# Weight loads of two attention groups on ScalarE's queue, and no cached-key steps in a group's first two row blocks

## The chip, the cores and the metric

One core of a Trainium2 chip runs the kernel. Its engines are TensorE (PE: matmuls, with its weight loads shown as PEld), VectorE (DVE), ScalarE (ACT), GpSimd (POOL) and SyncE (SP), which here only issues DMAs. Each engine works through its own list of instructions in order and waits where an instruction's operands aren't there. DMAs are issued by SP, ACT or POOL, wait in the issuer's list like any other instruction, and are carried by 16 DMA engines. The metric is the device time of one execution in microseconds, as the median of several runs.

## What is computed

One layer of a decoder on 1024 prompt rows and 8 x 8 sample rows, width 1024, all in float32:

```python
u = rmsnorm(x); a, q, k, v, g_a, g_b = split(u @ w_in)
# branch A: pooling over windows of 2/4/8/16 rows of a, a small linear map, @ w_pa
# branch B: attention in 3 head groups of 4 heads with (window, dilation)
#           (128, 1), (512, 4), (2048, 16); q and k are normed for each head
# a sample row attends to its group's cached keys and values as well:
#           out, lse = dilated_attention_sample(q, [cache_k, k], [cache_v, v], dil, band)
# the three groups' outputs are weighted by their softmax denominators, then @ w_pb
h = x + (sigmoid(g_a) * A + sigmoid(g_b) * B) @ w_o
y = h + relu(rmsnorm(h) @ w_up)**2 @ w_down
```

## The kernel before, in words

Every weight is split into a high and a low part in a reduced float32 form, and a product is made of three matmul passes. A weight panel of 2048 columns is brought by `panel` (L102): four raw pieces of 128 x 512 (256 KB) are loaded (L97 to L100), ScalarE copies the high part into `places` (L93), VectorE subtracts it from the raw piece for the low part (L94). All raw pieces of the kernel share three slots, so a piece can be loaded when the piece three before it has been split and subtracted. `places` holds three panels.

The attention stage runs the head groups in the order 2, 1, 0 (L932). Each group has three panels, for q, k and v, brought by `load(j)` (L959). For groups 1 and 0, `load(0)` and `load(1)` stand at the head of the group (L969, L970), `load(2)` behind the first q parts (L986); their splits are held back until given matmuls have ended, since they overwrite the panels of the group before. The row blocks follow: block 8 (the 64 sample rows) together with block 0, then blocks 1 to 5 alone, then 6 and 7. `qkv_part` (L522) makes q, k or v of a block: matmuls, then on ScalarE the squares for the norms (L557), on GpSimd the power (L561), on ScalarE the scale (L566). The attention of earlier blocks is put between these parts by a hand-written round of generators (`step`, L479).

The samples of group 2 attend to keys that lie 16 rows apart, so that each row has keys of its own. This work is cut into steps by the generator `sample_own_keys` (L733): a step loads a piece of the cache (`piece`, L724, 512 KB in two DMAs), multiplies the piece before it in four GpSimd products (L744 for keys, L768 for values) and reduces on VectorE (L746, or L771 and L772). There are 16 pieces of keys, one step for the softmax, 16 pieces of values, and 35 steps with the first load and the last sum. `own_step(1)` (L979) makes one step behind each part of each prompt block of groups 1 and 0; GpSimd's products are held until the matmuls before them have ended, the loads are not held. The generator's query tile `qs` is set up at the head of group 1 (L948 to L954). A finishing part on the samples (`sample_finish`, L868) starts when all steps are done.

TensorE's order is the program's. For the other engines, and for the queues of DMAs, a planner simulates the program ahead of time and orders the instructions by when they are ready, in the program's order among those that are; a load without a hold is put as early as its tile is free.

Of the kernel before, what the change touches and what calls it, by code (L numbers as in the profile page):

```python
# [10 lines left out]
ALU = mybir.AluOpType  # L11
# [4 lines left out]
P = 128  # L16
# [11 lines left out]
HD = 64  # L28
# [4 lines left out]
def decoder_step(ctx, tc, i, o):  # L33
    nc = tc.nc
    v_, s_, g_, t_ = nc.vector, nc.scalar, nc.gpsimd, nc.tensor
    dma = nc.sync.dma_start
# [60 lines left out]
    def raw_piece(src, name, a, load=dma):  # L97
        raw = rr(wp, [P, 512], F32, name=f"raw_{name}_{a}", tag="raw", bufs=3)
        load(raw, src[:, a:a + 512])
        return raw  # L100

    def panel(src, name, between=None, after=None, ahead=None):  # L102

        n = src.shape[1]
        wt = places[:, place[0] % 3]
        place[0] += 1
        for a in range(0, n, 512):
            raw = ahead.pop(0) if ahead else raw_piece(src, name, a)
            if between is not None:
                between(a // 512)  # L110
            ins = split(wt[:, 0, a:a + 512], wt[:, 1, a:a + 512], raw)
            if after is not None:
                behind_pe(ins, after[a // 512])
        throttle.append(ins)
        return wt
# [31 lines left out]
    new_d = [dp.tile([NT, NB, 768], F32, name=f"new_d{g}") for g in range(3)]  # L147
# [312 lines left out]
    ap = pb.enter_context(tc.tile_pool(name="att", bufs=1, reuse_waits="tile"))  # L460
# [50 lines left out]
    ends_of = {}  # L511
# [387 lines left out]
    own_keys = None  # L899
    count = [0]  # L900

    def own_step(every):
        count[0] += 1
        if count[0] % every == 0:
            if next(own_keys, True) is not None and (2, "own") not in done:
                done.add((2, "own"))
# [25 lines left out]
    for g in (2, 1, 0):  # L932
        nq = i["qk_norm"]
        if g == 1:
            assert ("p", 3) in done
            flush()
            pa.close()
            pam.close()
            ap2 = pb2.enter_context(tc.tile_pool(name="att2", bufs=1, reuse_waits="tile"))
            sp1 = psm.enter_context(tc.tile_pool(name="smp1", bufs=1, side="right", reuse_waits="tile"))  # L940
            np_ = psm2.enter_context(tc.tile_pool(name="nat", bufs=1, side="right", reuse_waits="tile"))
            sp = psm2.enter_context(tc.tile_pool(name="smp2", bufs=1, side="right", reuse_waits="tile"))
            osm = ap2.tile([P, 3, 4, 66], F32, name="osm")

            for a in range(2):
                v_.memset(osm[64:, a], 0.0)
                v_.memset(osm[64:, a, :, 64], -NEG)
            qs = sp1.tile([P, 768], F32, name="qs")  # L948
            for hf in range(2):
                dma(qs[64 * hf:64 * hf + 64], new_d[2].rearrange("t b c -> (t b) c"))  # L950
            wq = sp1.tile([P, 2, 256], F32, name="wq", tag="ss")[:, 0]
            dma(wq, bass.AP(tensor=nq.tensor, offset=nq.offset + 2 * 512, ap=[[0, P], [1, 256]]))
            v_.scalar_tensor_tensor(qs[:, :256], wq, HD ** -0.5, qs[:, :256], op0=ALU.mult, op1=ALU.mult)
            own_keys = sample_own_keys(qs)  # L954
        wrow = ap1.tile([P, 256], F32, name=f"wrow{g}", tag="wrow")
        dma(wrow, bass.AP(tensor=nq.tensor, offset=nq.offset + g * 512 + 256, ap=[[0, P], [1, 256]]))
        wts = [(place[0] + j) % 3 for j in range(3)]

        def load(j, *after):  # L959
            panel(i["w_in"][2 + 3 * j + g], f"qkv{g}_{j}", after=[ends_of[a] for a in after] or None)  # L960


        if g == 2:
            load(0)
            load(1)
            load(2)
        else:
            h = g + 1
            load(0, (h, 6, 1), (h, 7, 1), (h, 6, 2), (h, 6, 2))  # L969
            load(1, (h, 6, 2), (h, 7, 2), (h, 7, 2), (h, 7, 2))  # L970
        for blks in ((8, 0), (1,), (2,), (3,), (4,), (5,)) + (((6, 7),) if g else ((6,), (7,))):
            if g == 1 and 6 in blks:
                in_order(0)
            tiles = {b: qkv_tiles(f"{g}_{b}", b == 8) for b in blks}

            for js in (((0, 1), (2,)) if blks[0] in (1, 2, 3, 4, 5) else ((0,), (1,), (2,))):
                for b in blks:
                    qkv_part(g, wts, b, f"{g}_{b}", tiles[b], js)
                    if g < 2 and b < 8:  # L979
                        own_step(1)  # L980
                    if 2 in js:
                        (sample_block if b == 8 else prompt_block)(g, b, *tiles[b])
                if g == 2 and 2 in js and 8 in blks:
                    start(pool_branch(), "p", now=True)
                if g < 2 and 0 in js and 8 in blks:
                    load(2, (g, 8, 0), (g, 0, 0), (g, 0, 0), (g, 0, 0))  # L986


    while (2, "own") not in done:
# [68 lines left out]
    for d in range(4):  # L1058
# [7 lines left out]
        for u, (c, m) in enumerate(units):  # L1066
# [3 lines left out]
            name = f"{d}_{c}_{m}"  # L1070
# [663 lines left out]
```

## Time and profile before

| | us |
|---|---|
| median of 3 runs (1481.65 to 1486.06) | 1483.24 |
| the profiled execution's own time | 1482.97 |
| its span, first to last instruction | 1481.2 |

Busy shares of the span are 98% for TensorE, 94% for its weight loads, 68% for VectorE, 46% for ScalarE and 28% for GpSimd. A matmul's end is modelled, so a busy TensorE isn't one at its peak. The granted TensorE clock is a share of its full 2.4 GHz; 0.50 is the lower of its two levels, 1.2 GHz, and a mean between them says that part of the stretch was at either. The attention stage lies from about 55 to 430 us of the span: group 2 to about 174, group 1 to about 281, group 0 to about 409. A wait is idle time of an engine just before an instruction, put down to what came last.

### The profile page before, as it was taken

What the parts mean: (1) busy time and instruction counts of PE and PEld (TensorE: products, weight loads), DVE (VectorE), ACT (ScalarE), POOL (GpSimd) and SP (SyncE); (2) the same over time, 40 slices, a digit from 0 to 9 for tenths busy, and PEclk for the clock granted to TensorE, in tenths of its full rate; (3) what the DMA queues carried; (4) which work ended last, traced back from release to release, by engine and by line L of the source; (5) the groups of instructions that cost most, each with busy time, mean ns of one, the idle gap of its engine ahead of it and who ended that gap; (6) DMA issues with size and microseconds to landing.
All of it is one profiled execution on the core that took longest, in us unless ns stands there. A gap on an engine that the chain in (4) does not pass through costs nothing.

```text
span 1481.2 us, 28011 instructions
## 1 busy us (share of the span) xinstructions
PE 1446.0 (98%) x10595; PEld 1397.2 (94%) x10595; DVE 1009.2 (68%) x1949; ACT 687.8 (46%) x1885; POOL 412.5 (28%) x619
## 2 busy tenths in 40 slices
PE   8999899989999999999999999999998999999998
PEld 8988788878999999999998999999998999999998
DVE  7555555767864443434668989888987566777786
ACT  8466745667784222222346665655555322222220
POOL 1611246646500000010200121111224444544430
PEclk9999899999999999999999999999999999999999
DMA  6311767764456547468620777766768788567542
GB/s 216 98 47 63 194 139 174 211 182 119 119 146 201 197 163 258 163 203 287 249 101 27 286 265 265 277 247 254 265 246 306 297 345 322 227 273 277 216 189 113
DMA packets 124277, 304.72 MB, mean 206 GB/s; under 512 B 19111, under 2 KB 72045, under 8 KB 118830
## 3 DMA queue, kind: packets, MB, share of 16 engines
q1 hardware_dynamic: 102334, 192.27, 39.5%
q0 software_dynamic: 21376, 109.88, 20.4%
q8 instruction: 83, 1.36, 0.4%
q10 hardware_dynamic: 432, 0.79, 0.2%
q14 instruction: 52, 0.43, 0.1%
HBM read 218.49 MB, written 128.05 MB: 234 GB/s over the span
## 4 chain that ended last, share of the span: by engine, by line
PE 74%; issue 11%; DVE 5%; DMA 5%; POOL 3%; ACT 2%; SPq 0%; POOLq 0%; ACTq 0%; DVEq 0%
PE p1d L1202 12%; PE pga L136 6%; PE pgb L136 6%; PE pqk L136 6%; PE p2d L1202 6%; PE ph L136 6%; PE p1u L1202 5%; PE pv L136 4%; PE a L264 3%; PE pa L136 3%; PE p3d L1202 3%; PE p2u L1202 2%; POOL z_d L1335 2%; DMA raw_qkv<-in_w_in_dram 2%; DVE places L94 2%
## 5 line engine op out<-in xcount | busy, mean ns | idle before, releaser
L1202 PE MATMUL p1d<-act,places 128*128 128x272 f32 x1104 | 191.3, 288 | 3.9 <-DVE yd L1582 1.4
L1202 PEld LDWEIGHTS p1d<-act,places 128*128 128x128 f32 x1104 | 163.0, 188 | 5.4 <-DVE yd L1582 2.5
L1335 POOL DMA_DIRECT2D z_d<-zs_M x105 | 56.4, 537 | 245.6 <-DVE zs_M L94 242.4
L1632 POOL DMA_DIRECT2D out_kv_sample_dram<-in_cache_kv_dram x44 | 22.1, 505 | 317.6 <-ACT places L93 303.1
L1582 DVE TENSOR_TENSOR yd<-yd,p1d 128x544 f32<-128x544 f32 x116 | 83.1, 716 | 38.5 <-PE p1d L1202 38.4
L93 ACT ACTIVATE places<-sd 128x512 fp32r<-128x512 f32 x64 | 37.4, 625 | 143.7 <-issue 106.9
L1202 PE MATMUL p1u<-t,places 128*128 128x272 f32 x768 | 103.1, 291 | 0.7 <-ACT q L1449 0.7
L1202 PE MATMUL p1u<-act,places 128*128 128x272 f32 x768 | 102.2, 289 | 1.3 <-ACT q L1377 1.3
L1202 PEld LDWEIGHTS p1u<-t,places 128*128 128x128 f32 x768 | 99.7, 191 | 0.8 <-ACT q L1449 0.8
L1202 PEld LDWEIGHTS p1u<-act,places 128*128 128x128 f32 x768 | 98.6, 188 | 1.8 <-ACT q L1377 1.5
L136 PE MATMUL pga<-act,places 128*128 128x384 f32 (+1 forms) x576 | 98.0, 328 | 0.0
L136 PE MATMUL pgb<-act,places 128*128 128x384 f32 (+1 forms) x576 | 97.8, 326 | 0.0
L1202 PE MATMUL p2d<-act,places 128*128 128x272 f32 x528 | 93.9, 288 | 1.6 <-DVE places L94 1.0
L136 PEld LDWEIGHTS pgb<-act,places 128*128 128x128 f32 x576 | 95.4, 188 | 0.0
L136 PE MATMUL ph<-act,places 128*128 128x384 f32 (+2 forms) x624 | 95.4, 314 | 0.0
L136 PEld LDWEIGHTS ph<-act,places 128*128 128x128 f32 x624 | 95.3, 188 | 0.0
L136 PEld LDWEIGHTS pga<-act,places 128*128 128x128 f32 x576 | 94.6, 188 | 0.3
L561 POOL TENSOR_TENSOR mr<-ms,mhalf 128x4 f32<-128x4 f32 (+2 forms) x39 | 51.4, 1319 | 110.9 <-DVE ms L560 105.9
L93 ACT ACTIVATE places<-rd 128x512 fp32r<-128x512 f32 x64 | 37.1, 625 | 94.6 <-PE p1d L1202 94.6
L1202 PEld LDWEIGHTS p2d<-act,places 128*128 128x128 f32 x528 | 78.8, 188 | 2.3 <-DVE places L94 1.2
L1534 POOL TENSOR_TENSOR sd<-rd 128x128 f32<-128x128 f32 x64 | 38.6, 604 | 130.3 <-DVE places L94 115.7
L94 DVE TENSOR_TENSOR zs_M<-q,zs_M 128x544 fp32r<-128x544 f32 x75 | 54.0, 722 | 19.7 <-ACT zs_M L93 19.7
(383 smaller groups left out, 3673.1 us busy)
## 6 DMA issues: line engine op xcount, KB each, us to landing
z_d<-zs_M POOLq DMA_DIRECT2D x105, 544.0 KB, 4.4
act<-z_d SPq DMA_DIRECT2D x73, 544.0 KB
out_kv_sample_dram<-in_cache_kv_dram POOLq DMA_DIRECT2D x36, 960.0 KB, 7.4
ru<-in_w_up_dram SPq DMA_DIRECT2D x16, 1024.0 KB
rd<-in_w_down_dram SPq DMA_DIRECT2D x15, 1024.0 KB
raw_qkv<-in_w_in_dram SPq DMA_DIRECT2D x36, 256.0 KB
zc<-z_d SPq DMA_DIRECT2D x16, 544.0 KB
pck<-in_cache_kv_dram SPq DMA_DIRECT2D x32, 256.0 KB
```

The source lines that it names most:

```text
L93: ins = s_.activation(dst_hi, src, AF.Copy)
L94: v_.tensor_tensor(dst_lo, src, dst_hi.bitcast(F32), op=ALU.subtract)
L136: last_mm[0] = t_.matmul(out, lhs(a, k), rhs(b, k), start=(j == 0), stop=(j == len(terms) - 1))
L264: last_mm[0] = t_.matmul(pts[m][:, :n], wt[:, a, kk, m * P:(m + 1) * P], act4[b][kk][:, :, part4(c)], start=(p == 0 and kk == 0), stop=(p ...
L561: g_.tensor_tensor(r[:n, :H], ms[:n, :H], mhalf[:n, :H], op=ALU.pow)
L1202: last_mm[0] = t_.matmul(pt[:, s, :R4], w(a, k), z(b, k, s), start=(start and j == 0), stop=(j == len(terms) - 1), skip_group_check=True)
L1335: g_.dma_start(z_d[f][AT[m]], st.rearrange("p b l -> p (b l)").bitcast(F32))
L1534: ins = g_.tensor_tensor(s[:, 0], a21, a22, op=ALU.add)
L1582: v_.tensor_tensor(part, part, p[src], op=ALU.add)
L1632: ins = g_.dma_start(d, a)
```

## The change

`panel` takes the function that issues its loads. In groups 1 and 0 the 24 raw pieces of the six panels with a held split are issued by ScalarE instead of SP; group 2 and the later stages stay on SP. The call of `own_step` behind the three parts of block 0 is left out in both groups. One more step is made behind the value parts of blocks 2 and 4 in group 1 and of block 2 in group 0. The loads of `qs` and `wq`, the product on them and the start of the generator move from the head of group 1 to behind the key parts of its first two row blocks (8 and 0); the tiles are still taken at the head.

```diff
-    def panel(src, name, between=None, after=None, ahead=None):
+    def panel(src, name, between=None, after=None, ahead=None, load=dma):
...
-            raw = ahead.pop(0) if ahead else raw_piece(src, name, a)
+            raw = ahead.pop(0) if ahead else raw_piece(src, name, a, load)
...
             qs = sp1.tile([P, 768], F32, name="qs")
-            for hf in range(2):
-                dma(qs[64 * hf:64 * hf + 64], new_d[2].rearrange("t b c -> (t b) c"))
             wq = sp1.tile([P, 2, 256], F32, name="wq", tag="ss")[:, 0]
-            dma(wq, bass.AP(tensor=nq.tensor, offset=nq.offset + 2 * 512, ap=[[0, P], [1, 256]]))
-            v_.scalar_tensor_tensor(qs[:, :256], wq, HD ** -0.5, qs[:, :256], op0=ALU.mult, op1=ALU.mult)
-            own_keys = sample_own_keys(qs)
...
-            panel(i["w_in"][2 + 3 * j + g], f"qkv{g}_{j}", after=[ends_of[a] for a in after] or None)
+            panel(i["w_in"][2 + 3 * j + g], f"qkv{g}_{j}", after=[ends_of[a] for a in after] or None,
+                  load=nc.scalar.dma_start if after else dma)
...
-                    if g < 2 and b < 8:
+                    if g < 2 and 0 < b < 8:
                         own_step(1)
+                        if 2 in js and (g, b) in ((1, 2), (1, 4), (0, 2)):
+                            own_step(1)
...
                 if g < 2 and 0 in js and 8 in blks:
                     load(2, (g, 8, 0), (g, 0, 0), (g, 0, 0), (g, 0, 0))
+                if g == 1 and 1 in js and 8 in blks:
+                    for hf in range(2):
+                        dma(qs[64 * hf:64 * hf + 64], new_d[2].rearrange("t b c -> (t b) c"))
+                    dma(wq, bass.AP(tensor=nq.tensor, offset=nq.offset + 2 * 512, ap=[[0, P], [1, 256]]))
+                    v_.scalar_tensor_tensor(qs[:, :256], wq, HD ** -0.5, qs[:, :256], op0=ALU.mult, op1=ALU.mult)
+                    own_keys = sample_own_keys(qs)
```

## Rows read from the trace of the kernel before

**Rows 1.** TensorE's waits, 150 to 330 us: waiter, releaser: total us, times, longest.
```profile
PE pv L541 <- DVE places L94: 5.0, 4, 3.3
...
PE pv L538 <- ACT places L93: 2.3, 1, 2.3
PE sg1b L597 <- ACT ocg1b L631: 2.3, 1, 2.3
...
PE pq L541 <- DVE places L94: 2.0, 2, 1.4
...
PE pos L855 <- DMA vts<-in_cache_kv_dram: 1.5, 1, 1.5
...
PE tps L828 <- DVE pxs L822: 1.0, 1, 1.0
...
PE pog1b L628 <- ACT pTg1b L619: 0.7, 1, 0.7
```

**Rows 2.** Windows: length, busy us of PE, PEld, DVE, ACT, POOL; clock, DMA share, GB/s.
```profile
150.00:162.00 12.00, 12.00 (x99) 11.39 (x98) 5.89 (x20) 10.14 (x41) 2.02 (x2) 1.00 0.42 114
162.00:174.00 12.00, 12.00 (x106) 11.74 (x105) 7.86 (x23) 8.67 (x35) 1.88 (x2) 1.00 0.90 257
...
177.00:188.00 11.00, 6.02 (x27) 4.45 (x26) 4.87 (x11) 7.59 (x40) 2.42 (x3) 0.50 0.75 195
188.00:192.00 4.00, 4.00 (x24) 4.00 (x25) 1.08 (x9) 1.65 (x8) 0.00 (x0) 0.68 0.00 0
...
299.00:304.00 5.00, 5.00 (x30) 4.97 (x30) 3.59 (x16) 4.27 (x24) 1.78 (x2) 0.66 0.95 254
...
192.00:262.00 70.00, 70.00 (x542) 58.36 (x541) 39.14 (x116) 38.28 (x197) 39.33 (x49) 1.00 0.73 171
```

**Rows 3.** TensorE in time order: start, duration, instruction, count, [idle before <- releaser].
```profile
171.22 3.14 PE L136 MATMUL pk<-places,act 128*128 128x256 f32 x24
176.69 0.45 PE L538 MATMUL pv<-places,smp_t 128*128 128x256 f32 x1 [2.33 <-ACT places L93]
...
409.07 2.34 PE L136 MATMUL pga<-act,places 128*128 128x384 f32 x12
...
430.82 0.63 PE L896 MATMUL sft<-cst,sres 128*128 128x64 f32 x4
```

**Rows 4.** SP in time order; runs of one kind are merged, waits between them included.
```profile
152.38 8.79 SPq L99 DMA_DIRECT2D raw_qkv<-in_w_in_dram  x5
...
165.34 1.40 SPq L950 DMA_DIRECT2D qs<-new_d  x2
...
169.34 1.54 SPq L99 DMA_DIRECT2D raw_qkv<-in_w_in_dram  x3
...
177.99 7.56 SPq L99 DMA_DIRECT2D raw_qkv<-in_w_in_dram  x4
```

**Rows 5.** VectorE in time order.
```profile
163.45 0.69 DVE L94 TENSOR_TENSOR places<-raw_qkv,places 128x512 fp32r<-128x512 f32 x1
...
304.09 2.49 DVE L822 TENSOR_TENSOR pxs<-ps,cst 128x32 f32<-128x32 f32 x1 [0.94 <-ACT ps L817]
...
397.91 0.89 DVE L776 TENSOR_TENSOR osm<-osm,ss 128x256 f32<-128x256 f32 x2
```

**Rows 6.** The chain that ended last, in time order, pieces of loads: start, us, what.
```profile
159.36 3.17 DMA raw_qkv<-in_w_in_dram
...
169.34 6.65 DMA raw_qkv<-in_w_in_dram
...
177.99 5.83 DMA raw_qkv<-in_w_in_dram
```

**Rows 7.** Loads issued by ScalarE at the start: ns least/median/most, first and last start.
```profile
L99 ACTq DMA_DIRECT2D raw_a<-in_w_in_dram x3: 412/451/452, 0.7 to 1.7; - x3
```

**Rows 8.** GpSimd in time order.
```profile
221.91 5.59 POOL L744 TENSOR_TENSOR pck<-pck,qs 128x256 f32<-128x256 f32 x8 [5.96 <-DMA pck<-in_cache_kv_dram]
...
304.20 2.33 POOL L768 TENSOR_TENSOR pcv<-pcv,sc 128x256 f32<-128x256 f32 x4
```

## The prediction

> **What bounds the kernel now.** The page's busy shares put TensorE far ahead of the rest, so time can only be won where TensorE waits or runs at its lower clock. The list of who waited for whom, cut to the stretch of the three attention groups, names seven groups of waits [rows 1]; in the time order of TensorE all of them lie at the two changes of group, about 174 to 186 us and 281 to 318 us. Between these, from 192 to 262 us, TensorE is busy for 70.00 of 70 us [rows 2], while steps on the cached keys run all the time. So the change is worth what it does to two stretches, and can cost something in the blocks between them.
>
> *First change of group (2 to 1).* The key part of block 0 starts at 171.22 us and takes 3.14, to 174.36; the value part of the sample block starts at 176.69 after a wait of 2.33 for the split of the third panel [rows 3]. With the waits inside that part it is 2.3 + 5.0 = 7.3 us [rows 1]. The granted clock is 0.50 from 177 to 188 us and 0.68 to 192 us [rows 2]: the lower level of the two, after a stretch with waits. At half clock TensorE's 6.02 busy us hold 3.0 us of work, so 3.0 are lost, and 4.0 x 0.32 = 1.3 after that. Sum: **11.6 us**.
>
> Why is the panel late? Its first three pieces go out from 169.34 us, in SP's order behind the loads of qs (165.34), of two norm rows and of a cache piece [rows 4]. The slot of the first was free at 164.14, when VectorE had subtracted the piece three before it (163.45 + 0.69) [rows 5]: 5.2 us lost in SP's order. Then the load took 6.65 us, against 3.17 for the same size ten us earlier; the fourth piece needs the first one's slot, goes out at 177.99 and takes 5.83 [rows 6]. The DMA engines are busy at 0.90 in 162 to 174 us [rows 2].
>
> *Second change (1 to 0).* Five waits: 2.0 + 2.3 + 1.5 + 1.0 + 0.7 = 7.5 us [rows 1], and 5 us at clock 0.66 [rows 2], 1.7 lost: **9.2 us**. Together at most 20.8 us are to be had.
>
> **Part 1: 24 weight pieces go from SP's queue to ScalarE's.** At the first change the first piece no longer stands behind SP's loads. It is out at 164.14 + 0.45, the duration of the same load issued by ScalarE at the kernel's start [rows 7]. Landing takes 3.17 to 6.65 [rows 6]: 167.8 to 171.2. Split and subtraction are some 0.7 each (0.69 for the second [rows 5]; the first is taken as equal), so the slot is free at 169.2 to 172.6; the fourth piece is out 0.45 later, takes 3.17 to 5.83, and with its own 1.4 it is there at 174.2 to 180.3. TensorE wants it three quarters into a sample part: 16 matmuls at the rate of 24 in 3.14 [rows 3] are 2.1 us, so at 174.36 + 1.6 = 175.9. A wait of 0 to 4.4 us stays. I take 2.0, about the middle, since the engines stay nearly full but the queue is no longer shared, and suppose that the clock doesn't fall for so little. Gain 11.6 - 2.0 = **9.6** (7.2 to 11.6).
>
> The rows show a piece that takes 6.65 us behind other loads of its queue and 3.17 before them [rows 6]; that it is the queue is my reading. The Trainium skill (DMA: Bandwidth & Descriptors, "Issuing engines are not separate DMA queues") speaks against it: DMAs of all issuing engines run on the same 16 DMA engines, and another issuer saves only the time of issuing. By that rule the pieces keep 6.65 and 5.83 and the gain is 7.2 in place of 9.6. No row here shows two such queues at once.
>
> What the edit adds lies on ScalarE: 24 issues x 0.45 = 10.8 us [rows 7], half in each change of group. ScalarE is busy for 10.14 + 8.67 = 18.8 of the 24 us from 150 to 174 [rows 2], which leaves 5.2 us for the 9 issues that fall there (4.1). They hide, barely; without that cover they cost up to 5.4 in each change. Each issue also waits in ScalarE's order for its slot, and behind it stand the norms' squares and scales, the exponentials and the copies out of PSUM, for which TensorE's transposes and products wait. I charge **0.5**; the case where these waits are long is a rival below. On SP nothing is added, and what stood behind its weight loads goes out earlier.
>
> **Part 2: no steps in blocks 8 and 0 of groups 1 and 0, one more at three later blocks.** A step is four GpSimd products, 5.59 / 2 = 2.8 us [rows 8], a VectorE pass and a 512 KB load (two SP issues). 35 steps are needed. Before there are 19 calls in each group, three of them at block 0; after there are 18 and 17, so the last step comes with the last block of group 0.
>
> At the second change VectorE's product of the sample's probabilities takes 2.49 us from 304.09 on, for a 128x32 operand [rows 5], beside GpSimd's products of 304.20 to 306.53 [rows 8]: it waits there rather than works. With the step gone, TensorE's 1.0 behind it goes. The two waits behind ScalarE (2.3 and 0.7) come of ScalarE standing in front of a raw piece; two value loads leave that stretch, so pieces land sooner, but the waits for slots come to ScalarE. I take half of 2.3 + 0.7 + 1.7 (clock): 2.4. The 2.0 of the first panel stays (blocks 6 and 7 keep their steps just before it), and the 1.5 for a load of cached values. Gain **3.4** (-2 to 9.2; below nothing if the 5.4 us of issues all lie in the way).
>
> The cost: the steps crowd. At the three blocks with an added step two come at once. The nearest row is a pair that already runs without a gap, eight products in 5.59 us at 221.91 [rows 8], in the stretch where TensorE waits for nothing [rows 2]. Bounds 0 and, if TensorE stands for one step at each, 3 x 2.8 = 8.4; I take **0.5**, near the row.
>
> The end: the sum over the cached values was done at 397.91 + 0.89 [rows 5] and TensorE reads what comes of it at 430.82 [rows 3]. It now waits for the last block, whose end is near 409.07, where the first gate begins [rows 3]; with a step's 2.8 us and VectorE's sums it still has some 15 us of cover: nothing. qs is set up behind the sample's key part and is wanted only in block 1: nothing; without that cover its loads would hold GpSimd's first products, not TensorE.
>
> **Sum.** 9.6 + 3.4 - 0.5 - 0.5 = 12.0 us off the profiled execution, 1482.97 us (span 1481.2 and 1.8 around it), which is 0.3 below the median of 1483.24: **1471 us**. Late next are the fourth piece of group 1's third panel and the first panel of group 0. The gates and the MLP behind are TensorE's own chain and move forward as they are.
>
> **The rivals.**
> *Bandwidth, not the queue (the change doesn't clear the way).* The planner sends loads that have no pace as early as it can, so qs and two cache pieces may still fill 162 to 177 us although their step stands later in the program. For it: the share of 0.90 [rows 2]. Against it: the 5.2 us in SP's order go in any case. 7.2 in group 1, nothing in group 0, 1.0 of cost: 6.2 off, 1476.8.
> *Crowded steps.* GpSimd waits for a load between paired steps, the norms' power behind it is late, and TensorE stands at three blocks: 1471 + 8.4, about 1479.4, within 0.3%. Against it: the pair of [rows 8].
> *ScalarE held (slower).* An issue waits for its slot in ScalarE's own order. On SP five issues took 8.79 us at 152.38, and four 7.56 us at 177.99 [rows 4]; without some 0.34 each for the issues that is 7.1 + 6.2 = 13.3 us of waiting in one change of group. If ScalarE sits there, with 5.4 of issues it needs 18.7 us and has 5.2: 13.5 late, past the 11.6 to be won, and in group 0 the same 13.5 against 9.2. Sum 1.9 + 4.3 = 6.2 slower, about 1489. It decides once ScalarE waits for slots for more than some 11 us in each change. Against it: on SP, pieces that nothing hurried made most of that waiting.
>
> **How the numbers follow.** Forecast 0.55 (its own range 1464 to 1478), bandwidth 0.20, crowded steps 0.12, ScalarE held 0.13. A measurement of this kernel can tell about 0.3%, 4.4 us, from no change; faster is below 1478.8. Of the four cases 0.54, 0.15, 0.04 and 0 lie there: 0.73. Within: 0.01 + 0.05 + 0.07 + 0.03 = 0.16. Slower: 0.01 + 0.10 = 0.11. The range goes from 20 us off (nearly all of the 20.8) into the crowded case: 1463 to 1481.
>
> **What would show it.** Right: no fall of the granted clock at 177 us; weight pieces issued by ScalarE within 0.5 us of their slot; the sample's value part within 2 us of the key part's end; no GpSimd products in the first two blocks of groups 1 and 0; TensorE without waits from block 1 on. Wrong: raw pieces that still take 6 us; ScalarE idle in front of issues; norms' scales late behind paired steps.

## The result and the profile after

The changed kernel takes 1495.75 us (median of 6 runs, 1490.67 to 1496.91) where the kernel before took 1483.74 beside it (1479.98 to 1486.06): a ratio of 1.0081, with an interval of 1.0065 to 1.0097. It is slower, by some 12 us, where 12 us of gain were forecast. The profiled execution's span went from 1481.2 to 1495.1 us.

Where the time came is read best from the drift of TensorE: the start of the same matmuls in both traces, after less before. The first place lies ahead of the change; the five others cut the stretch into the parts that the prediction priced.

| start of | before, us | after, us | drift | part that ends there | its share |
|---|---|---|---|---|---|
| value parts of blocks 6 and 7, group 2 | 153.6 | 153.9 | +0.3 | all that comes before | +0.3 |
| value part of block 0, group 1 | 187.9 | 187.0 | -0.9 | first change of group | -1.2 |
| value part of block 7, group 1 | 277.7 | 283.5 | +5.8 | blocks of group 1 | +6.7 |
| value part of block 1, group 0 | 324.8 | 330.1 | +5.3 | second change of group | -0.5 |
| value part of block 7, group 0 | 405.5 | 413.6 | +8.1 | blocks of group 0 | +2.8 |
| the samples' sums (L896) | 430.8 | 445.0 | +14.1 | end of attention, first gates | +6.0 |

Each drift is that of one execution. At 153.6 us, ahead of all edits, the traces of the kernels shown below differ by up to 1.1 us from that of before, and this is taken off the first share. after and after_short (below), whose edits are alike up to block 6 of group 0, differ by 1.5 us in their first share, so a share under some 2 us in one kernel alone isn't read.

TensorE's waits of after from 150 to 440 us answer to [rows 1] (waiter, releaser: total us, times, longest):

```profile
PE pv L541 <- DVE places L94: 7.0, 2, 4.9
PE pos L855 <- DMA vts<-in_cache_kv_dram: 3.0, 2, 2.1
PE sg1b L597 <- ACT ocg1b L631: 2.4, 1, 2.4
PE pog1b L628 <- ACT pTg1b L619: 1.9, 1, 1.9
PE tpg0b L616 <- ACT ocg0b L631: 1.8, 1, 1.8
PE tcg0b L720 <- DVE ocg0b L654: 1.5, 1, 1.5
PE sg1b L597 <- DVE ps L815: 1.4, 1, 1.4
```

The wait for the split of the third panel is still there (7.0 in place of 5.0 and 2.3). New are the one behind ps, one more for a load of cached values, and those for tpg0b and tcg0b. That of pog1b has grown from 0.7 to 1.9, and the one behind pxs is gone. The windows of after answer to [rows 2] (length, busy us of PE, PEld, DVE, ACT, POOL; clock, DMA share, GB/s):

```profile
162.00:174.00 12.00, 12.00 (x106) 11.74 (x104) 6.04 (x18) 7.52 (x26) 1.00 (x1) 1.00 0.91 259
174.00:188.00 14.00, 6.31 (x37) 5.03 (x36) 8.64 (x34) 10.61 (x56) 3.01 (x3) 0.73 1.10 215
192.00:262.00 70.00, 66.42 (x488) 54.44 (x487) 35.57 (x107) 34.65 (x185) 37.02 (x47) 0.98 0.56 146
...
400.00:440.00 40.00, 36.21 (x284) 34.43 (x284) 30.11 (x103) 28.59 (x91) 15.58 (x20) 0.96 0.53 141
```

The stretch from 192 to 262 us, which had been full [rows 2], has lost 3.6 us of work; at the end, where GpSimd is busy for 15.58 us, TensorE stands for 3.8 of 40. The DMA share in 162 to 174 us is 0.91, as it was (0.90).

*The first change of group.* The third panel in after; ACTq and SPq are the two issuers of DMAs:

```profile
166.60 0.33 ACTq L99 DMA_DIRECT2D raw_qkv<-in_w_in_dram  x1
...
169.03 2.00 SPq L798 DMA_DIRECT2D kts<-in_kT_dram  x2
...
173.08 1.99 SPq L730 DMA_DIRECT2D pck<-in_cache_kv_dram  x2
173.09 0.63 ACT L93 ACTIVATE places<-raw_qkv 128x512 fp32r<-128x512 f32 x1 [4.07 <-DMA raw_qkv<-in_w_in_dram]
...
174.52 0.34 ACTq L99 DMA_DIRECT2D raw_qkv<-in_w_in_dram  x1
...
176.65 0.37 SPq L798 DMA_DIRECT2D kts<-in_kT_dram  x1
177.13 2.27 SPq L730 DMA_DIRECT2D pck<-in_cache_kv_dram  x2
...
182.94 0.63 ACT L93 ACTIVATE places<-raw_qkv 128x512 fp32r<-128x512 f32 x1 [1.02 <-DMA raw_qkv<-in_w_in_dram]
...
184.35 0.47 PE L541 MATMUL pv<-places,smp_t 128*64 128x256 f32 x1 [4.90 <-DVE places L94]
```

The first piece goes out at 166.60 in place of 169.34 [rows 4] and lands 6.5 us later, at 173.09; the fourth goes out at 174.52 and takes 8.4 us, with TensorE behind it. Beside them SP sends three loads of the samples' keys and two cached pieces (four DMAs), though the steps that the pieces belong to now stand a block later: nothing holds loads, and the planner still puts them here. In before the two pieces had gone out 5 to 6 us earlier, all ahead of the fourth piece (177.99 [rows 4]):

```profile
167.89 1.35 SPq L730 DMA_DIRECT2D pck<-in_cache_kv_dram  x2
...
170.96 0.60 SPq L730 DMA_DIRECT2D pck<-in_cache_kv_dram  x1
```

Now the fourth piece, 3.5 us earlier itself, is under way together with them.

*The blocks of group 1.* What the first added step, behind the value part of block 2, leads to:

```profile
219.75 5.60 POOL L744 TENSOR_TENSOR pck<-pck,qs 128x256 f32<-128x256 f32 x8 [4.37 <-PE sg1b L597]
...
223.87 7.35 SPq L730 DMA_DIRECT2D pck<-in_cache_kv_dram  x4
...
228.77 2.81 POOL L744 TENSOR_TENSOR pck<-pck,qs 128x256 f32<-128x256 f32 x4 [3.42 <-DMA pck<-in_cache_kv_dram]
231.61 1.22 DVE L746 TENSOR_REDUCE sc<-pck 128x16 f32<-128x1024 f32 x1 [0.60 <-POOL pck L744]
232.72 0.98 SPq L846 DMA_DIRECT2D vts<-in_cache_kv_dram  x2
232.75 0.29 DVE L815 TENSOR_TENSOR ps<-pss,ps 128x136 f32<-128x136 f32 x1
...
233.09 0.71 PE L597 MATMUL sg1b<-qkTg1b 64*128 64x128 f32 x6 [1.44 <-DVE ps L815]
```

There are two slots for cached pieces. The two steps use up both pieces that are there, eight products without a gap (219.75). The next piece goes out only at 223.87, when the slot of the first of them has come free; SP sends its two DMAs and the two of the piece behind it, the last when the second slot comes free, and sits there for 7.35 us with the samples' value loads behind it (232.72). GpSimd waits 3.42 us for the next step's piece; VectorE's sum of it stands in VectorE's order ahead of the samples' scores (L815), for which TensorE waits, by now in block 4. Behind the pair at block 4 the value loads are late again: TensorE waits 2.14 us for one at 254.07, in block 5.

*The end.* GpSimd and ScalarE in after:

```profile
417.71 2.53 POOL L768 TENSOR_TENSOR pcv<-pcv,sc 128x256 f32<-128x256 f32 x4 [2.36 <-DMA pcv<-in_cache_kv_dram]
420.20 1.00 POOL L561 TENSOR_TENSOR mr<-ms,mhalf 128x4 f32<-128x4 f32 x1
...
421.24 0.93 ACT L566 ACTIVATE qk<-pk,mr 128x64 f32<-128x64 f32 x4 [3.27 <-POOL mr L561]
```

The last step's products wait 2.36 us for their piece and stand in GpSimd's order ahead of the power for the norms of the last block (mr); ScalarE waits 3.27 us for that, and the last block's attention, transposes and exponentials all come later. VectorE's order is in the way too: the product that tcg0b waits for (L654) starts at 417.64, straight behind a sum of the steps (L772, 417.04 to 417.72).

### The profile page after: what moved, and what is told of

Its sections match the earlier page's. It is cut to its first block, busy times and chain, and to the rows that moved or that the text cites. A ratio compares the mean times of both kernels' runs of the same rounds, so it can differ in the third digit from the quotient of the medians.

```text
span 1495.1 us, 28003 instructions
## 1 busy us (share of the span) xinstructions
PE 1451.7 (97%) x10595; PEld 1400.4 (94%) x10595; DVE 1009.3 (68%) x1949; ACT 686.4 (46%) x1885; POOL 412.6 (28%) x619
## 4 chain that ended last, share of the span: by engine, by line
PE 60%; issue 18%; DMA 6%; POOL 6%; DVE 5%; ACT 3%; SPq 0%; POOLq 0%; ACTq 0%; DVEq 0%
PE p1d L1206 11%; PE ph L136 6%; PE pgb L136 6%; PE pga L136 6%; PE p2d L1206 5%; PE pqk L136 4%; POOL z_d L1339 3%; PE a L264 3%; PE pv L136 3%; PE pa L136 3%; PE p3d L1206 2%; DMA raw_qkv<-in_w_in_dram 2%; PE pb L136 2%; DVE places L94 1%; DMA pck<-in_cache_kv_dram 1%
## 5 line engine op out<-in xcount | busy, mean ns | idle before, releaser
L93 ACT ACTIVATE places<-s_M 128x512 fp32r<-128x512 f32 x64 | 40.1, 628 | 57.9 <-PE p1u L1206 32.7
```

What stands on the lines that cost most here:

```text
L93: ins = s_.activation(dst_hi, src, AF.Copy)
```

## The experiments

All runs are set against the kernel before on the same chip. The drift of each at the six places, in us:

| kernel | 153.6 | 187.9 | 277.7 | 324.8 | 405.5 | 430.8 | median against before | ratio, interval |
|---|---|---|---|---|---|---|---|---|
| after | +0.3 | -0.9 | +5.8 | +5.3 | +8.1 | +14.1 | 1495.75, 1483.74 | 1.0081 [1.0065, 1.0097] |
| queue_only | +1.1 | +0.3 | +1.2 | -0.4 | -0.4 | -0.6 | 1481.02, 1481.86 | 0.9992 [0.9977, 1.0007] |
| steps_only | +0.1 | -2.7 | +6.0 | +6.0 | +9.7 | +14.9 | 1496.66, 1481.86 | 1.0096 [1.0067, 1.0124] |
| steps_g1 | -0.3 | -4.0 | +1.5 | +0.4 | +0.5 | +3.1 | 1489.45, 1481.86 | 1.005 [1.0032, 1.0068] |
| after_hold | -0.2 | -4.1 | +5.1 | +6.1 | +7.9 | +11.9 | 1493.54, 1481.86 | 1.0086 [1.0067, 1.0104] |
| g1_nodouble | +0.4 | -4.5 | -4.9 | -3.4 | -3.3 | +0.8 | 1483.32, 1482.42 | 1.0007 [0.9994, 1.0019] |
| doubles_only | -0.7 | -1.7 | +5.1 | +2.1 | +3.7 | +3.5 | 1489.49, 1482.42 | 1.0057 [1.0033, 1.0081] |
| end_late | +0.3 | +0.7 | +1.0 | -2.4 | -2.4 | +2.3 | 1484.31, 1482.42 | 1.0015 [1.0001, 1.0029] |
| g0_doubles | -1.1 | -5.0 | -4.7 | -5.9 | -3.2 | -2.0 | 1482.13, 1482.42 | 1.0009 [0.9997, 1.0021] |
| clear_sp | -1.1 | -11.2 | -11.7 | -9.4 | -6.3 | -5.1 | 1477.43, 1481.76 | 0.9966 [0.995, 0.9982] |
| clear_act | +0.1 | -8.7 | -9.8 | -8.4 | -5.7 | -4.4 | 1478.78, 1481.76 | 0.9981 [0.9963, 1.0] |
| work_noload | +0.3 | +0.8 | +3.2 | +1.8 | +1.9 | +1.7 | 1484.48, 1481.76 | 1.0011 [0.9999, 1.0024] |
| after_short | +0.6 | -2.1 | +4.5 | +4.5 | +6.9 | +6.8 | 1492.41, 1481.76 | 1.0064 [1.0041, 1.0088] |

The ratio is that on record for the runs and not the quotient of the two medians. A drift stands for one execution and the median for all: steps_g1 is 3.4 us longer than before in the span of its trace and 7.6 in the medians, g0_doubles 4.1 shorter and 0.3. At the first change steps_only, steps_g1, g1_nodouble and g0_doubles, whose edits are alike up to there, win between 2.7 and 4.9 us (from 153.6 to 187.9).

**queue_only: the kernel before with part 1 alone.**

```diff
-            panel(i["w_in"][2 + 3 * j + g], f"qkv{g}_{j}", after=[ends_of[a] for a in after] or None)
+            panel(i["w_in"][2 + 3 * j + g], f"qkv{g}_{j}", after=[ends_of[a] for a in after] or None,
+                  load=nc.scalar.dma_start if after else dma)
```

> Only the weight pieces of groups 1 and 0 go to ScalarE's queue; the steps on the cached keys stay as in the kernel before. Theory A (the steps' part of the change costs: their loads sit on the DMA engines while the panel's last piece is loaded, and they crowd into fewer blocks): about the time of the kernel before, 1481 to 1486 us. Theory B (ScalarE's queue costs: issues wait for slots in ScalarE's order and hold the norms and exponentials): most of the 12 us of loss, 1491 to 1497 us.

No difference, 0.9992 [0.9977, 1.0007]. The issues take 0.33 to 0.34 us each and cost nothing that can be seen; nor do they win anything:

```profile
167.48 0.34 ACTq L99 DMA_DIRECT2D raw_qkv<-in_w_in_dram  x1
...
172.50 0.63 ACT L93 ACTIVATE places<-raw_qkv 128x512 fp32r<-128x512 f32 x1
...
174.04 0.43 DVE L953 SCALAR_TENSOR_TENSOR qs<-wq,qs 128x256 f32<-128x256 f32 x1 [2.86 <-DMA wq<-in_qk_norm_dram]
176.80 0.68 DVE L94 TENSOR_TENSOR places<-raw_qkv,places 128x512 fp32r<-128x512 f32 x1
...
177.83 0.33 ACTq L99 DMA_DIRECT2D raw_qkv<-in_w_in_dram  x1
...
184.20 0.63 ACT L93 ACTIVATE places<-raw_qkv 128x512 fp32r<-128x512 f32 x1 [4.40 <-DMA raw_qkv<-in_w_in_dram]
```

The first piece is out 1.9 us earlier than before, but the fourth at 177.83 (before: 177.99 [rows 4]). Two things hold it. The first piece takes up to 5.0 us, to its split at 172.50; and VectorE, which stands 2.86 us in front of the product on qs for the load of wq, subtracts it only from 176.80. The fourth then takes 6.4 us on a queue that carries weight pieces alone. TensorE's longest wait there is 5.4 us.

**steps_only: the change with its weight pieces left on SP** (part 2 alone).

```diff
-                  load=nc.scalar.dma_start if after else dma)
+                  load=dma)
```

> Only the steps' part of the change; all weight pieces stay on SP's queue. Theory A (the steps' part costs): 1490 to 1497 us, with TensorE's waits in blocks 3 to 5 of group 1 and at the end of group 0 as in the changed kernel. Theory B (ScalarE's queue costs): 1478 to 1485 us, and those waits gone.

1.0096 [1.0067, 1.0124], with its losses in the same three parts as after (8.7, 3.7 and 5.2 us in place of 6.7, 2.8 and 6.0). The whole loss is part 2's.

**steps_g1: part 2 in group 1 alone**, on SP. Group 0 keeps its steps at block 0 and gets no added one; the last step comes behind the query part of block 7.

```diff
-                    if g < 2 and 0 < b < 8:
+                    if g < 2 and (0 if g == 1 else -1) < b < 8:
                         own_step(1)
-                        if 2 in js and (g, b) in ((1, 2), (1, 4), (0, 2)):
+                        if 2 in js and (g, b) in ((1, 2), (1, 4)):
```

> The steps' part in group 1 alone, on SP's queue: no step at block 0 of group 1, one more at its blocks 2 and 4; group 0 keeps its 19 calls, so the steps end one block earlier than in the changed kernel. Theory A, crowding in both groups: the 6 us of group 1 stay and the 6 us at the end of group 0 go, 1486 to 1491 us. If the end costs nothing by itself, it is like the kernel with the whole steps' part. Theory B (ScalarE's queue costs): 1478 to 1485 us.

The loss of 5.5 us in group 1's blocks stays, that of 2.8 in group 0's goes, and the end costs 2.6 in place of 6.0. At the first change SP sends the first piece at 165.92, earlier than ScalarE does in after, since the loads of qs now stand behind it; it lands within 4.5 us. The fourth piece goes out as soon as its slot is free, ahead of the cached pieces on the same queue, and takes 8.0 us all the same:

```profile
171.84 0.34 SPq L99 DMA_DIRECT2D raw_qkv<-in_w_in_dram  x1
172.22 0.69 SPq L730 DMA_DIRECT2D pck<-in_cache_kv_dram  x1
...
179.87 0.63 ACT L93 ACTIVATE places<-raw_qkv 128x512 fp32r<-128x512 f32 x1 [1.89 <-DMA raw_qkv<-in_w_in_dram]
```

**after_hold: the change with four early loads held.** The loads of qs wait for the sample's and block 0's value parts, those of the first two cached pieces for the matmuls ahead of their step.

```diff
-            dma(t[64 * hf:64 * hf + 64], a)
+            ins = dma(t[64 * hf:64 * hf + 64], a)
+            if kv == 0 and j < 2 * KPC:
+                behind_pe(ins)
...
-                if g == 1 and 1 in js and 8 in blks:
+                if g == 1 and 2 in js and 8 in blks:
                     for hf in range(2):
-                        dma(qs[64 * hf:64 * hf + 64], new_d[2].rearrange("t b c -> (t b) c"))
+                        behind_pe(dma(qs[64 * hf:64 * hf + 64], new_d[2].rearrange("t b c -> (t b) c")))
```

> The changed kernel with the loads of the samples' queries and of the first two pieces of cached keys held until the matmuls of group 1's first blocks have ended, so that they can't be in flight beside the last raw piece of the third panel. Theory A1 (the full DMA engines decide when that piece lands): it lands in 3 to 5 us in place of 8.4, TensorE's 7.7 us of waiting at the first change of group fall to 1 to 3, and the clock doesn't fall there; the steps start later and crowd more, so the whole is 1487 to 1494 us. Theory B (ScalarE's order decides): the waiting at the first change stays at 6 to 8 us, 1494 us or more.

The first change wins 3.9 us, no more than steps_g1 did without a hold (3.6): the samples' key loads and wq still go out among the first pieces, 162 to 174 us still has a DMA share of 0.86, and the first piece takes 6.9 us. The fourth, with little beside it (a share of 0.35 from 174 to 188 us), takes at most 5.4. After it 9.2 us are lost in group 1's blocks, the most of all kernels.

**g1_nodouble: steps_g1 without its two added steps.** The last step is behind the value part of block 7.

```diff
-                        if 2 in js and (g, b) in ((1, 2), (1, 4)):
-                            own_step(1)
```

> Steps left out at block 0 of group 1 alone, no step added anywhere: 16 calls in group 1 and 19 in group 0, so the last step comes behind the value part of block 7 of group 0. All weight pieces on SP. Against steps_g1 this takes away the two added steps of group 1 and moves the end of the steps two parts later. Doubles theory: the loss of some 5 us that steps_g1 had between the value part of block 3 and block 7 of group 1 comes from the two added steps; without them it is under 2 us, TensorE stands about -2 us against the kernel before at the end of group 1 in place of +1.5, and the late end then takes 5 to 6 us from 405 us on: in all +3 to +5 us. Shift theory: the loss comes from all steps of the group coming three parts later (a load of cached keys meets the sample's value loads), the doubles being free: the loss stays 4 to 6 us, and in all +6 to +9 us. No-end theory (the loss behind 405 us in the changed kernel is not from the late last step): the drift stays as it is from 392 us on.

The drift stays at -4.5 to -4.9 us through all of group 1: the loss there is that of the added steps and not of the steps' later start. The late end takes 4.1.

```profile
192.00:262.00 70.00, 70.00 (x554) 59.06 (x553) 36.24 (x122) 37.89 (x201) 36.97 (x46) 1.00 0.59 153
400.00:440.00 40.00, 36.63 (x277) 35.07 (x276) 29.84 (x111) 30.11 (x80) 7.39 (x10) 1.00 0.40 115
```

GpSimd has as much to do from 192 to 262 us as in after (36.97 and 37.02 us), but TensorE doesn't stand.

**doubles_only: the kernel before with the three added steps.** The steps at block 0 stay; the last one is behind the value part of block 5.

```diff
                     if g < 2 and b < 8:
                         own_step(1)
+                        if 2 in js and (g, b) in ((1, 2), (1, 4), (0, 2)):
+                            own_step(1)
```

> The kernel before with the three added steps (value parts of blocks 2 and 4 of group 1 and of block 2 of group 0) and with the steps at block 0 kept, so the steps end early, behind the value part of block 5 of group 0. First change of group untouched (drift 0 up to 210 us). Doubles theory: +3 to +6 us in group 1, some 1 us in group 0, nothing at the end (the last three parts of group 0 have no steps): in all +3 to +6 us. Shift theory: within 1.5 us of the kernel before. My prediction charged the three pairs with 0.5 us in all, with bounds of 0 and 8.4.

6.8 us in group 1's blocks for two pairs, 1.6 in group 0's for one, nothing at the end. The first pair:

```profile
224.45 7.00 SPq L730 DMA_DIRECT2D pck<-in_cache_kv_dram  x4
...
229.53 2.81 POOL L744 TENSOR_TENSOR pck<-pck,qs 128x256 f32<-128x256 f32 x4 [3.60 <-DMA pck<-in_cache_kv_dram]
...
233.86 1.22 PE L597 MATMUL sg1b<-qkTg1b 64*128 64x128 f32 x6 [1.73 <-DVE ps L815]
```

The same rows as in after. With these waits the granted clock falls: it is 0.89 from 224 to 240 us, where it had been 1.00.

**end_late: the kernel before without the steps at block 0 of group 0**, nothing added; the last step is behind the value part of block 7.

```diff
-                    if g < 2 and b < 8:
+                    if g < 2 and (-1 if g == 1 else 0) < b < 8:
```

> The kernel before with the steps at block 0 of group 0 left out and nothing added: 19 calls in group 1, 16 in group 0, the last one behind the value part of block 7. Group 1 and the first change of group are untouched (drift 0 up to 281 us). It shows the second change by itself and the late end by itself. Theory of the late end: TensorE gains 1 to 3 us between 299 and 325 us (the prediction gave 3.4 for the second change), loses 0 to 1 us in blocks 1 to 6, and 5 to 6 us between 405 and 434 us: in all +2 to +5 us. As predicted (15 us of cover at the end): -1 to -3.5 us in all, no loss behind 405 us.

The second change wins 3.4 us, the end loses 4.7. Not all of the 3.4 need be the steps': work_noload and queue_only, which keep them there, win 1.3 and 1.6 in that part. GpSimd's power is late here as in after:

```profile
410.77 0.93 ACT L566 ACTIVATE qk<-pk,mr 128x64 f32<-128x64 f32 x4 [2.98 <-POOL mr L561]
```

**g0_doubles: no steps at block 0 of group 1, the three missing ones as pairs in group 0.** On SP; the last step is behind the value part of block 6, as in the kernel before.

```diff
-                    if g < 2 and 0 < b < 8:
+                    if g < 2 and (0 if g == 1 else -1) < b < 8:
                         own_step(1)
-                        if 2 in js and (g, b) in ((1, 2), (1, 4), (0, 2)):
+                        if 2 in js and (g, b) in ((0, 1), (0, 3), (0, 5)):
```

> Steps left out at block 0 of group 1, the three that are missing added behind the value parts of blocks 1, 3 and 5 of group 0, so that the last step comes behind the value part of block 6 of group 0, where it was before. All weight pieces on SP. If doubles in group 1 and the late end are what the change loses: the gain of 4 us at the first change stays, blocks 1 to 7 of group 1 lose under 2, the three pairs in group 0 lose 0 to 3, nothing behind 405 us: in all -4 to +1 us. If the steps' shift is what costs in group 1: +1 to +5 us.

2.7 us for three pairs in group 0, 0.9 each, where a pair in group 1 costs 3.4. The gain of the first change (4.0) is kept up to group 0. The median doesn't differ from before (1.0009), although the profiled execution, the fastest of the ten, is 4.1 us shorter in span.

**clear_sp: g0_doubles with the first change cleared.** The loads of qs and wq wait for the key part of block 0, the first two cached pieces for its value part, and the samples' first four key loads (two rounds of two) for a matmul of block 1.

```diff
+                    if (g, b) == (1, 0) and 2 in js:
+                        holds[0] = last_mm[0]
...
+            if kv == 0 and j < 2 * KPC:
+                behind_pe(ins, holds[0])
...
+                    if g == 1 and bg == 0 and r < 2:
+                        holds[1] = holds[1] or last_mm[0]
+                        behind_pe(ins, holds[1])
...
-                        dma(qs[64 * hf:64 * hf + 64], new_d[2].rearrange("t b c -> (t b) c"))
-                    dma(wq, bass.AP(tensor=nq.tensor, offset=nq.offset + 2 * 512, ap=[[0, P], [1, 256]]))
+                        behind_pe(dma(qs[64 * hf:64 * hf + 64], new_d[2].rearrange("t b c -> (t b) c")))
+                    behind_pe(dma(wq, bass.AP(tensor=nq.tensor, offset=nq.offset + 2 * 512, ap=[[0, P], [1, 256]])))
```

> g0_doubles with every other load of the first change of group held: the loads of qs and wq behind the key part of block 0, the first two pieces of cached keys and the sample's first three loads of keys behind the value part of block 0 (about 187 us). The third panel of group 1 is left alone on SP with the results' stores. Bandwidth theory: what made its pieces take 5 to 8 us were the other loads, on whatever queue; the first and the last piece now land within 3.5 us, TensorE waits under 1.5 us between 174 and 188 us, and the gain at the value part of block 0 goes from 4 to 5 us to 8 to 11 us. Other theory: the pieces were late for another reason (their slots, the split on ScalarE and VectorE): the gain stays at 4 to 6 us. Later blocks: the steps' first loads come some 14 us later, so 0 to 3 us may be lost again in blocks 1 to 4. In all -1 to -8 us against the kernel before.

The drift at 187.9 us is -11.2, and 10.1 us of it are won at the first change; 1477.43 us in all: 0.9966 [0.995, 0.9982], faster than either kernel, with the weight pieces on SP.

```profile
165.00 5.50 SPq L99 DMA_DIRECT2D raw_qkv<-in_w_in_dram  x4
...
168.79 0.63 ACT L93 ACTIVATE places<-raw_qkv 128x512 fp32r<-128x512 f32 x1 [1.08 <-DMA raw_qkv<-in_w_in_dram]
...
173.50 0.67 ACT L93 ACTIVATE places<-raw_qkv 128x512 fp32r<-128x512 f32 x1
```

```profile
162.00:174.00 12.00, 12.00 (x106) 11.67 (x103) 8.45 (x28) 10.92 (x43) 2.01 (x2) 1.00 0.68 222
174.00:188.00 14.00, 13.88 (x94) 11.84 (x93) 6.30 (x29) 9.59 (x57) 2.01 (x2) 1.00 0.66 169
```

The four pieces stand in a row in SP's order; the first lands within 3.8 us, the fourth (out by 170.5) before 173.5. TensorE is busy for 13.88 of 14 us at a clock of 1.00. Nothing of it is lost in group 1; 5.4 us are given back up to 405 us, 2.3 at the second change and 3.1 in group 0's blocks with pairs.

**clear_act: clear_sp with the pieces on ScalarE's queue.**

```diff
-                  load=dma)
+                  load=nc.scalar.dma_start if after else dma)
```

> clear_sp with the 24 weight pieces on ScalarE's queue. With nothing else in the way of the pieces the queue theory of the prediction has least to win and ScalarE's issues remain: within 1 us of clear_sp at the first change of group if the queue is neutral by itself; 2 us better if a queue of its own still helps; 2 us or more worse if the issues in ScalarE's order cost.

8.8 us won at the first change, 1.3 less than in clear_sp, and in all 0.9981 [0.9963, 1.0]. The first piece takes 4.6 us, the fourth at most 3.8. A queue of its own wins nothing even here; whether it costs the 1.3 isn't shown, since kernels that are alike differ by as much.

**work_noload: the work of two pairs without their loads.** Two steps of the kernel before multiply and sum their piece twice.

```diff
+            for n in range(KPC if j in (20, 36) else 0):
+                behind_pe(g_.tensor_tensor(t[:, n], t[:, n], qs[:, :256], op=ALU.mult))
             yield
+            for _ in range(2 if j in (20, 36) else 1):
-            behind_pe(v_.tensor_reduce(...))
+                behind_pe(v_.tensor_reduce(...))
```

> The kernel before, in which the steps behind the value parts of blocks 2 and 4 of group 1 make their four GpSimd products twice and their VectorE sum twice (pieces 5 and 9 of the keys are multiplied twice, so the samples' outputs of group 2 are not the reference's). It has the engines' work of two added steps and none of their loads; the steps end where they did before. Load theory: in the pairs TensorE waits because the second piece can only be loaded when the first one's slot is free, and SP stands in front of it with the sample's loads behind it: without the load the loss in group 1 is under 2 us, in place of the 6.7 us of doubles_only. Work theory: GpSimd's and VectorE's own time in the pair (2.8 and 1.2 us) is what makes the sample's work late: the loss stays 4 to 7 us.

2.4 us lost in group 1's blocks, against 6.8 in doubles_only. That lies between the two theories and nearer to that of the load: some third of a pair's price would be the engines' work, and two thirds come with the second load. TensorE's waits from 200 to 281 us are down to

```profile
PE pss L816 <- DMA kts<-in_kT_dram: 0.5, 1, 0.5
PE sg1b L597 <- DVE ps L818: 0.3, 1, 0.3
```

**after_short: the change without its last three pieces of cached values**, so that its steps end behind block 6 of group 0.

```diff
-        for j in js:
+        for j in js[:13]:
             t = loaded.pop()
-            if j + KPC < 64:
+            if j + KPC < 52:
```

> The changed kernel with the last three pieces of cached values left out (32 steps; the samples' outputs of group 2 lack these values), so that its steps end behind the value part of block 6 of group 0, as in the kernel before. Late-end theory: of the 6 us that the changed kernel loses from 405 to 434 us against the kernel before, 4 to 6 go; the blocks before are as in the changed kernel (+5 to +6 us at the end of group 1, +7 to +8 in block 6 of group 0); in all +6 to +9 us against the kernel before. If the end loses for another reason (the gates' panels, the drift itself): the drift at 434 us stays near +14.

The 6.0 us of the end are gone (+6.9 at 405.5, +6.8 at 430.8):

```profile
400.00:440.00 40.00, 40.00 (x326) 38.80 (x326) 28.94 (x109) 33.16 (x100) 5.21 (x6) 1.00 0.35 103
```

TensorE is full from 400 to 440 us again, with GpSimd at 5.21 us in place of 15.58.

## Why the prediction was wrong

**Part 1, gain 9.6 forecast: 1.2 came.** The step that failed is "I take 2.0, about the middle, since the engines stay nearly full but the queue is no longer shared". Its bounds for the fourth piece, 3.17 to 5.83 us, were those of [rows 6]; it took 8.4, above both. The reading of [rows 6] behind it, that a piece is slow because it stands behind other loads of its queue, is refuted from three sides: queue_only gives the pieces another queue and wins nothing (there VectorE's wait for wq has a part in it); in steps_g1 the fourth piece goes out ahead of the cached pieces of its queue and still takes 8.0 us; clear_sp leaves the pieces on SP, takes the other loads away, and wins nearly all. That was the rival *Bandwidth, not the queue*; but its price, 7.2, kept the 5.2 us in SP's order as a sure gain. They weren't one: the first piece kept what it won (out 2.7 us earlier, landed 2.9 earlier), but the fourth, for which TensorE waits, did not (out 3.5 earlier, landed 0.9 earlier), since it now met the cached pieces. Nor did the earlier start need a second queue: part 2, which moves the loads of qs, gives it to SP (steps_g1), and steps_only, part 2 without part 1, wins 2.7 us here where after wins 1.2. The rule weighed against the change (the Trainium skill, DMA: Bandwidth & Descriptors, "Issuing engines are not separate DMA queues": all issuers' DMAs run on the same 16 engines and interleave) stands: the trace agrees, with 0.9992 for the queue alone.

The steps' loads did not move with the steps. They came only 5 to 6 us later, beside the fourth piece (DMA share 0.91, then 1.10 from 174 to 188 us); the planner's rule on loads without a hold, which the prediction named under its rival, decided. The stretch itself was sized nearly right: 11.6 us to be had, 10.1 won in clear_sp.

**ScalarE's issues, 0.5 forecast: not contradicted.** They take 0.33 to 0.38 us, a little less than the 0.45 of [rows 7], and queue_only shows no cost within its interval, some 2 us. In after they come 1.3, 0.3, 0.3 and 0.1 us behind their slots. *ScalarE held*, the slower rival, was not what happened: where ScalarE stands, it waits for a piece to land (4.07 us).

**Crowded steps, 0.5 forecast: 6.7 in group 1 and 2.8 in group 0.** The step that failed is the row chosen for a pair. The eight products without a gap in [rows 8] show two steps whose pieces were both there. So it is in after too (219.75); what the pair delays is the next piece, since calling two steps at once also means two loads at once, with two slots. The upper bound, one step's 2.8 us for each block, was nearer: 3.4 a pair in group 1 (doubles_only), 0.9 to 3.7 in group 0 (g0_doubles, steps_only). Steps that come one by one cost nothing, with GpSimd as busy as in after (g1_nodouble). work_noload puts 2.4 of the 6.8 down to the work, and the rest to the load: SP held in front of the slot, the samples' loads behind it, VectorE's sum ahead of the samples' scores. So the rival *Crowded steps* had GpSimd's wait for a load and nearly the price, 8.4 for 9.5. Its other half, a late power for the norms, is not what TensorE waited for in group 1: that was the samples' scores and value loads. Its time, 1479.4, was wrong because it left the other terms as forecast.

**The end, 0 forecast: 6.0.** The step that failed is "it still has some 15 us of cover": it looked at who reads the steps' result. Nobody waited for that: the last sum (L776) is done at 423.92 + 0.43 = 424.35, TensorE reads at 444.95. The cost is in GpSimd's and VectorE's order, where the last steps' work stands in front of the last block's norms and attention. Over the kernels of the table it goes by the place of the last step: behind the value part of block 7 4.0 to 6.0 us (after, steps_only, after_hold, g1_nodouble, end_late), behind the query part of block 7 2.6 (steps_g1), behind block 6 or earlier 1.4 or less (the others). Taking three pieces away brings it to nothing (after_short).

**The second change, gain 3.4 forecast: 0.5.** The 1.0 behind pxs is gone in after, as forecast. The step that failed is "two value loads leave that stretch, so pieces land sooner", by which the two waits behind ScalarE and the clock's loss were to be halved: the copy that the longer one waits for (ocg1b, L631) stands behind a split for whose piece ScalarE waits 2.3 us in after (at 304.84) and 1.2 in before (at 297.45). The two waits are 2.4 and 1.9 us in place of 2.3 and 0.7, a new one of 1.3 stands in front of pss (at 302.51, behind a subtraction on VectorE), and the clock from 300 to 320 us is 0.91 (before 0.92). end_late, which changes only that, shows 3.4, but the other kernels scatter there between a gain of 3.0 (doubles_only, which keeps the steps at block 0) and a loss of 2.3 (clear_sp, which keeps them too), and with the steps left out after, steps_only, after_hold and after_short win between 0.5 and -1.0. In clear_sp TensorE waits 4.1 us for the split of group 0's first panel, in before 2.0. What decides between them stays open; the steps at block 0 aren't it alone.

**The sum.** Forecast -9.6 - 3.4 + 0.5 + 0.5 + 0 = -12.0; come in the trace -1.2 - 0.5 + 0 + 9.5 + 6.0 = +13.8 (with the 0.3 from ahead of the change +14.1), in the medians +12.0. Of the signs listed, these failed: the clock fell (0.73 from 174 to 188 us), pieces took 6.5 and 8.4 us, TensorE waited in blocks 4 and 5 of group 1, and norms' scales came late behind the last steps. No GpSimd products in the first two blocks was right.

## What to carry to other kernels

A late load is read together with all that the DMA engines carry while it is under way; giving it another issuer moved its issue, and holding the loads that nobody needed yet moved its landing. Work that is moved out of a crowded stretch has to go where its slots, not only its engine, are free: one step at a time cost nothing here, two at a time 3.4 us in group 1. And the cover of work at the end of a stage is not the time until its result is read, but what stands behind it in its engines' orders.

## What the runs showed of the hardware

A load of the second queue is not served ahead of the first queue's. From 172 to 186 us of after, the DMA queues are

```profile
q1 hardware_dynamic: 2944, 2.10, 79.3%
q10 hardware_dynamic: 507, 0.93, 32.0%
```

(packets, MB, the time their packets took as a share of 16 engines). q10 is ScalarE's and carries the weight pieces; the shares add up to more than the whole, which is why the window reads 1.10. In that time the piece of 256 KB sent at 174.52 took 8.4 us, at 218 GB/s in all. In before, on one queue, the same 14 us have a share of 0.90 and 225 GB/s. In clear_sp, with one queue and the stretch from 162 to 174 us at a share of 0.68, the engines moved 222 GB/s; the first piece took 3.8 us and the fourth at most 3.3. So a higher share did not mean more bytes, which I hadn't expected. What is moved differs as well: 2985 of 3452 packets are under 2 KB in after's stretch, 1087 of 1787 in clear_sp's, and no run parts that from the number of queues.

Nor is a load that goes out first on its queue served alone: the fourth piece of steps_g1, ahead of four DMAs for cached pieces on SP, took 8.0 us, and at most 3.3 in clear_sp, where these and the other loads around it are held.
